# Seven block products instead of eight in the second feed-forward's up projection

## The chip, the cores and the metric

The kernel runs on one core of a Trainium2 chip. The time is the device time of one execution in microseconds; lower is better. TensorE (PE) multiplies matrices into PSUM, VectorE (DVE), ScalarE (ACT) and GpSimd (POOL) work on SBUF, the first two also on PSUM, and SyncE (SP) issues the loads.

## The reference

Two layers of a transformer over 512 latent tokens and 256 context tokens, model width 1024, float32. The first layer mixes by a state-space branch and attention, the second by latent attention (MLA); each ends with a gated feed-forward. What the change touches is the feed-forward of the second layer, which has only the 512 latent tokens:

```python
def swiglu(h, w_up, w_down):
    g, u = jnp.split(h @ w_up, 2, axis=-1)
    return (jax.nn.silu(g) * u) @ w_down
...
        x = x + mods[2] * o_lat
        h = modulate(rmsnorm(x, norm2_g[i]), mods[3], mods[4])
        x = x + mods[5] * swiglu(h, ffn_w_up[i], ffn_w_down[i])
...
    return rmsnorm(x, final_norm_g)
```

`w_up` is 1024 x 5632 (gate and up, 2816 hidden columns each), `w_down` is 2816 x 1024.

## The kernel before, in words

**Split products.** Every float32 matmul is made of three on TensorE: an operand is split into a high part (a copy rounded to the matmul's format, made by ScalarE) and a low part (the difference, made by VectorE or GpSimd), and high x high, high x low and low x high are added up in PSUM. For activations `Kern.split` does this (`L499`, `L500`; tiles `hh`, `hl`), for weights `WStream.split` (`L150` copies the loaded tile `wr` to `wh`, `L151` writes the difference `wl`; which engine does that alternates by the string `pat`).

**The weight stream.** `WStream` holds a plan of weight pieces in the order of their use. `dma` loads a piece of 128 x 1024 floats (512 KB), `split` makes its pair `wh`, `wl`. `lim(nraw, nhl)` says how many loaded pieces and how many pairs may be held; `free` gives a pair back and `pump` then loads and splits what comes next. All these tiles come from one pool of 14 buffers (`fp`).

**The second feed-forward** (`ffn` with `nt` = 4, called at the end of `phase_b`) goes through 11 blocks of 256 hidden columns, called pairs here (two tiles of 128 each), in four parts: (0, 1), (2, 3, 4), (5, 6, 7), (8, 9, 10). For each pair and each of its tiles `mm_w` fills two PSUM banks, one of gate and one of up, over eight contraction tiles, three matmuls each (`L662`, `L663`, `L665`), with the weight as stationary and all 512 tokens as moving operand. Pair 0 alone is done in two halves of 256 tokens, so that it can start when the first tokens are normalized. `act` then takes Silu of the gate (`L1248`), multiplies by up from PSUM (`L1249`) and splits the product into `hh` and `hl`. At the end of a part `out_gemm` multiplies these with the part's share of `w_down` (`gemm_t`, `L521` to `L523`) and adds the result, times a gate, to `x` (`L1188`, `L1189`); four matmul groups of the next part's first pair are started before it. After the last part, `final` normalizes and stores.

**Order.** The Python code names the instructions; a scheduler that simulates times puts them in order for each engine when the kernel is built, and on the chip every engine keeps this order. So an instruction that depends on nothing can be moved far ahead of its place in the code.

**Around it.** Before the feed-forward stands the attention output product, whose second half ends with `begin_norm` (normalize, transpose by `L248`, scale and shift by `L490`, split). The MLA stage earlier warms up the Exp table of ScalarE in `mla_in` (`L1325`), and its attention begins with `L1040`.

Of the kernel before, what the change touches and what calls it, by code (L numbers as in the profile page):

```python
# [18 lines left out]
P = 128  # L19
# [88 lines left out]
class WStream:  # L108
# [2 lines left out]

    def __init__(self, k, name):
        self.k, self.name = k, name
        self.plan = []
        self.raw, self.hl, self.rows = {}, {}, {}
        self.nd = self.ns = 0
        self.nraw, self.nhl = 2, 4
        self.live = 0
        self.pat = "P"
        self.stop = 1 << 30  # L120

    def add(self, srcs):
        i = len(self.plan)
        self.plan.extend(srcs)
        return list(range(i, len(self.plan)))

    def dma(self):
        src = self.plan[self.nd]
        t = self.k.f([P] + list(src.shape[1:]), F32, "wr")
        if isinstance(src, Halves):  # L130
            src.load(self.k.nc, t)
        else:
            self.k.nc.sync.dma_start(t, src)
        self.raw[self.nd] = t
        self.nd += 1

    def split(self):
        k, nc = self.k, self.k.nc
        i = self.ns
        if i >= self.nd:  # L140
# [12 lines left out]
        self.live += 1  # L153
        self.ns += 1
# [5 lines left out]
    def pump(self):  # L160
        while True:
            go = False
            while self.nd < min(len(self.plan), self.stop + self.nraw) and len(self.raw) < self.nraw:
                self.dma()
                go = True
            if self.ns < self.nd and self.live < self.nhl and self.ns < self.stop:
                self.split()
                go = True
            if not go:
# [14 lines left out]
class Kern:  # L184
# [393 lines left out]
    def plan_ffn(self, l):  # L578
        a, W, bp = self.a, self.W, self.block_pieces
        up, dn = a["ffn_w_up"][l], a["ffn_w_down"][l]  # L580
        pre = []
        for p, pairs in enumerate(FFN_PARTS):
            for j in pairs:
                gs = bp(up, 0, KD, 256 * j, 256, 4)
                self.i_up[l, j] = (pre + W.add(gs[len(pre):]), W.add(bp(up, 0, KD, HID + 256 * j, 256, 4)))
                pre = []
            if p + 1 < len(FFN_PARTS):

                pre = W.add(bp(up, 0, KD, 256 * FFN_PARTS[p + 1][0], 256, 4)[:1])
            self.i_dn[l, p] = [W.add(bp(dn, 2 * pairs[0], 2 * len(pairs), 512 * i, 512, 2)) for i in range(2)]  # L590

    def first_h(self):
# [708 lines left out]
            yield from self.out_gemm(hh, hl, 0, self.i_dn[l, p], range(nt), gate, after() if last else None)  # L1301


    def cq_at(self, s, i, t):
        return self.cqT[s][t // 2][:, i, (t % 2) * P:(t % 2 + 1) * P]

# [287 lines left out]
    def phase_b(self):  # L1594
# [51 lines left out]
        drive(self.out_gemm(self.oh, self.ol, 4, self.i_mo[1], range(NL), gate, self.begin_norm(1, 3)))  # L1646
        self.oh = self.ol = None
# [127 lines left out]
```

## Time and profile before

| | us |
|---|---|
| three timed runs | 2144.48, 2141.44, 2143.94 (median 2143.94) |
| the profiled execution's own time | 2144.06 |
| its span | 2142.1 |
| TensorE busy | 2053.3 (96%) |
| VectorE busy | 1217.9 (57%) |
| ScalarE busy | 842.9 (39%) |
| GpSimd busy | 798.9 (37%) |

Busy shares are averages over all stages. The second feed-forward runs from 1763 us to 2134 us of the span; what it waits for is read from that stretch alone. A matmul's row gives a start and a modelled duration that overlaps the next matmul; the distance of starts is what it costs in a stream.

### The profile page before, as it was taken

How to read it: one execution, taken by the hardware profiler on the slowest of the kernel's cores; microseconds unless marked ns; L12 is line 12 of the kernel's file. 1: busy time of each engine (PE TensorE's matmuls, PEld its weight loads, DVE VectorE, ACT ScalarE, POOL GpSimd, SP SyncE). 2: the span in 40 equal slices, each digit the busy share in tenths (PEclk: the TensorE clock that was granted, in tenths of full speed). 3: DMA queues.
4: the chain of work that ended last, by engine and by line, in shares of the span. 5: the costliest groups of instructions: out<-in, count | busy, mean ns of one | idle time of the engine just before them, and what ended most of it. 6: DMA issues, size and time to landing. Idle time of an engine off the chain costs nothing. (4 is left out here: it accounts for less than half of the span.)

```text
span 2142.1 us, 29547 instructions
## 1 busy us (share of the span) xinstructions
PE 2053.3 (96%) x11420; PEld 1689.4 (79%) x11420; DVE 1217.9 (57%) x2119; ACT 842.9 (39%) x1717; POOL 798.9 (37%) x701
## 2 busy tenths in 40 slices
PE   6999999999999899999999999999999999999998
PEld 3777777777777677888888878889888878888886
DVE  5699887867665697845345252175655663322223
ACT  4466554335665234312212212254555644222222
POOL 3456544575322355432232222254110154333333
PEclk9999999999999999999999999999999999999999
DMA  8211102410000641433335442112000033233232
GB/s 287 59 30 40 30 21 89 153 40 20 1 1 30 237 147 60 148 118 114 97 114 158 148 128 91 58 48 56 15 12 30 30 94 103 90 99 100 86 98 69
DMA packets 127574, 179.53 MB, mean 84 GB/s; under 512 B 16189, under 2 KB 77770, under 8 KB 127434
## 3 DMA queue, kind: packets, MB, share of 16 engines
q1 hardware_dynamic: 127434, 177.64, 26.3%
q8 instruction: 90, 1.47, 0.3%
q14 instruction: 50, 0.41, 0.1%
HBM read 172.35 MB, written 5.27 MB: 83 GB/s over the span
## 5 line engine op out<-in xcount | busy, mean ns | idle before, releaser
L151 POOL TENSOR_TENSOR wl<-wr,wh 128x1024 fp32r<-128x1024 f32 (+3 forms) x125 | 303.4, 2429 | 399.1 <-ACT wh L150 285.4
L150 ACT ACTIVATE wh<-wr 128x1024 fp32r<-128x1024 f32 (+3 forms) x211 | 218.5, 1037 | 517.4 <-DMA wr<-in_ffn_w_up_dram 126.2
L663 PE MATMUL gu<-hl,wh 128*128 128x512 f32 (+1 forms) x768 | 287.9, 375 | 1.5 <-POOL hl L500 1.5
L665 PE MATMUL gu<-hh,wl 128*128 128x512 f32 (+1 forms) x768 | 288.5, 376 | 0.4 <-DVE wl L151 0.4
L662 PE MATMUL gu<-hh,wh 128*128 128x512 f32 (+1 forms) x768 | 288.6, 377 | 0.0
L409 DVE SCALAR_TENSOR_TENSOR acc<-wa,sst,acc 128x512 f32<-128x512 f32 (+1 forms) x196 | 182.8, 975 | 88.1 <-DMA wa<-in_ada_w_dram 88.0
L151 DVE TENSOR_TENSOR wl<-wr,wh 128x1024 fp32r<-128x1024 f32 (+3 forms) x86 | 116.2, 1351 | 168.1 <-ACT wh L150 144.3
L521 PE MATMUL g<-wh,hh 128*128 128x512 f32 (+2 forms) x520 | 199.3, 384 | 0.5 <-DVE gt L1188 0.5
L522 PE MATMUL g<-wl,hh 128*128 128x512 f32 (+2 forms) x520 | 198.2, 381 | 0.0
L523 PE MATMUL g<-wh,hl 128*128 128x512 f32 (+2 forms) x520 | 197.2, 381 | 0.0
L1188 DVE TENSOR_TENSOR gt<-g,gate 128x512 f32<-128x512 f32 x132 | 90.3, 687 | 181.0 <-PE g L523 177.2
L662 PEld LDWEIGHTS gu<-hh,wh 128*128 128x128 f32 x768 | 144.4, 188 | 30.2 <-issue 2.8
L500 POOL TENSOR_TENSOR hl<-sg,hh 128x768 fp32r<-128x768 f32 (+1 forms) x44 | 71.8, 1631 | 249.3 <-ACT hh L499 249.1
L1038 DVE TENSOR_REDUCE nm<-S 128x1 f32<-128x768 f32 (+1 forms) x160 | 134.9, 848 | 45.5 <-PE S L1488 26.6
L663 PEld LDWEIGHTS gu<-hl,wh 128*128 128x128 f32 x768 | 144.8, 189 | 17.3 <-POOL hl L500 1.7
L665 PEld LDWEIGHTS gu<-hh,wl 128*128 128x128 f32 x768 | 144.9, 189 | 16.2 <-DVE wl L151 0.6
L1040 ACT ACTIVATE Pm<-S,nm 128x768 f32<-128x768 f32 (+1 forms) x160 | 130.2, 815 | 32.7 <-DVE nm L1038 32.0
L1189 POOL TENSOR_TENSOR x<-x,gt 128x512 f32<-128x512 f32 x66 | 90.6, 1378 | 132.1 <-DVE gt L1188 122.9
L248 PE MATMUL PTp<-ident,Pm 128*128 128x128 f32 x832 | 123.6, 276 | 6.1 <-ACT qT L1019 2.9
L248 PEld LDWEIGHTS PTp<-ident,Pm 128*128 128x128 f32 x832 | 96.1, 140 | 23.6 <-issue 10.4
L521 PEld LDWEIGHTS g<-wh,hh 128*128 128x128 f32 x520 | 97.6, 188 | 20.0 <-DVE gt L1188 1.0
L523 PEld LDWEIGHTS g<-wh,hl 128*128 128x128 f32 x520 | 97.7, 188 | 19.4
(308 smaller groups left out, 4657.9 us busy)
## 6 DMA issues: line engine op xcount, KB each, us to landing
wa<-in_ada_w_dram SPq DMA_DIRECT2D x96, 512.0 KB, 4.8
wr<-in_ffn_w_up_dram SPq DMA_DIRECT2D x88, 512.0 KB, 3.6
wr<-in_ffn_w_down_dram SPq DMA_DIRECT2D x44, 512.0 KB, 3.9
wr<-in_ab_w_in_dram SPq DMA_DIRECT2D x36, 512.0 KB, 3.7
wr<-in_ab_w_out_dram SPq DMA_DIRECT2D x16, 512.0 KB, 5.1
wr<-in_mla_w_o_dram SPq DMA_DIRECT2D x8, 512.0 KB, 3.7
yscr<-y SPq DMA_DIRECT2D x12, 256.0 KB, 2.6
yr<-yscr SPq DMA_DIRECT2D x6, 512.0 KB, 3.9
```

Source lines behind the costliest of these rows:

```text
L150: nc.scalar.activation(hi, raw, AF.Copy)
L151: eng.tensor_tensor(lo, raw, r32(hi), op=ALU.subtract)
L248: self.nc.tensor.transpose(out, in_, self.ident[:n, :n])
L409: nc.vector.scalar_tensor_tensor(acc[:, v], in0=raw[:, kk], scalar=c, in1=acc[:, v], op0=ALU.mult, op1=ALU.add)
L521: nc.tensor.matmul(ps, h, wh[:, kk, :], start=(n == 0), stop=False)
L522: nc.tensor.matmul(ps, h, wl[:, kk, :], start=False, stop=False)
L523: nc.tensor.matmul(ps, l, wh[:, kk, :], start=False, stop=(n == nk - 1))
L662: nc.tensor.matmul(o, a, hi[:, c0:c1], start=st, stop=False)
L663: nc.tensor.matmul(o, a, lo[:, c0:c1], start=False, stop=False)
L665: nc.tensor.matmul(o, b, hi[:, c0:c1], start=False, stop=sp)
L1038: nc.vector.tensor_reduce(nm, sp[:, 0:nb, 0:w], axis=AX.XY, op=ALU.max, negate=True)
L1040: nc.scalar.activation(p[:, 0:nkt * P].rearrange("p (a b) -> p a b", a=nb), sp[:, 0:nb, 0:w], AF.Exp, bias=nm, accum_out=u["sum"][:, ti, a ...
```

## The change

The up product of a pair is a product of two matrices that are each cut into 2 x 2 blocks: activations by tokens (256 + 256) and contraction (512 + 512), weights by contraction and by gate and up. Instead of eight block products the changed kernel makes seven, of sums and differences of blocks (Strassen's way, in the form with the fewest sums), and combines them. Pair 0 is computed as before; the ten others are changed.

- `begin_norm_q` takes the place of `begin_norm`: the normalized activations are kept whole (`hf`) and split by blocks ("11", "12", "21", "22": token half and contraction half). `sums_q` makes the four sums S1 to S4 in the course of pair 0, eight VectorE operations, and splits them.
- `WStream.seven` and `add_steps` plan seven steps for the four loaded pieces of a pair; `operand` makes the sum that a step needs on VectorE, in place, and `split` makes the pair from it. The low part of step n is written by the engine `PAT7[n]`: GpSimd for 0, 3, 5, VectorE for 1, 2, 4, 6.
- `up7` runs the seven products, 24 matmuls of 256 columns each (`mm_q`), and `ev` reads them out of PSUM: two copies on ScalarE, five additions on VectorE, the rest in SBUF.
- `ffn_q` takes the place of `ffn`. The stream may hold at most 14 buffers (`cap`), first 4 loaded pieces and 5 pairs, then 6 and 4 (before: 1 and 6). A Silu of one element is meant to load the table early.

```diff
+PAT7 = "PVVPVPV"
...
+    def operand(self, q, n):
+
+        a, b, d, c = (self.raw.get(i) for i in q["at"] + [None] * (4 - len(q["at"])))
+        V, G = self.k.nc.vector, self.k.nc.gpsimd
+        if n == 1:
+            V.tensor_tensor(b, d, b, op=ALU.subtract)
+        elif n == 2:
+            V.tensor_tensor(b, b, a, op=ALU.add)
+        elif n == 4:
+            V.tensor_tensor(a, d, b, op=ALU.subtract)
+        elif n == 5:
+            V.tensor_tensor(b, c, b, op=ALU.subtract)
+        for i in ((), (), (), (), (0,), (1, 3), (2,))[n]:
+            del self.raw[q["at"][i]]
+        return (a, b, b, c, a, b, d)[n]
...
-        raw = self.raw.pop(i)
+        raw = self.operand(q, n) if q else self.raw.pop(need)
         hi = k.f(list(raw.shape), F32R, "wh")
         lo = k.f(list(raw.shape), F32R, "wl")
-        eng = nc.gpsimd if self.pat[i % len(self.pat)] == "P" else nc.vector
+        pat = PAT7[n] if q else self.pat[i % len(self.pat)]
+        eng = nc.gpsimd if pat == "P" else nc.vector
...
+    def sums_q(self):
+
+        V, G = self.nc.vector, self.nc.gpsimd
+        self.quarters(("S1", "S2", "S3"))
+        for tt in range(2):
+            h1, h2 = self.hf[tt], self.hf[2 + tt]
+            a11, a12, a21, a22 = h1[:, 0:4], h1[:, 4:8], h2[:, 0:4], h2[:, 4:8]
+            V.tensor_tensor(a22, a21, a22, op=ALU.add)
+            V.tensor_tensor(a21, a11, a21, op=ALU.subtract)
+            self.split_q(a21, "S3", tt, G)
+            V.tensor_tensor(a11, a22, a11, op=ALU.subtract)
+            self.split_q(a11, "S2", tt, V)
+            self.split_q(a22, "S1", tt, G)
+            V.tensor_tensor(a12, a12, a11, op=ALU.subtract)
+            self.split_q(a12, "S4", tt, V)
+        self.hf = None
+
+    def mm_q(self, outs, i, name, start, stop):
+
+        nc = self.nc
+        wh, wl = self.W.get(i)
+        (h3, h1), (l3, l1) = self.q[name]
+        for o, m0 in outs:
+            for kk in range(4):
+                hi, lo = (h3[:, kk], l3[:, kk]) if kk < 3 else (h1, l1)
+                st, sp = start and kk == 0, stop and kk == 3
+                a, b = wh[:, kk, m0:m0 + P], wl[:, kk, m0:m0 + P]
+                nc.tensor.matmul(o, a, hi, start=st, stop=False)
+                nc.tensor.matmul(o, a, lo, start=False, stop=False)
+                nc.tensor.matmul(o, b, hi, start=False, stop=sp)
...
+    def up7(self, ids, hh, hl):
...
+        def ev(n, ps):
+            if n == 0:
+                t["p1"] = two(self.med(512, "hf"))
+                nc.scalar.activation(t["p1"], ps, AF.Copy)
+            elif n == 1:
+                t["w"] = self.e([P, 2, 2, 256], F32, "w7")
+                nc.scalar.activation(t["w"][:, 1], ps, AF.Copy)
+            elif n == 2:
+                t["u2"] = two(self.med(512, "hf"))
+                V.tensor_tensor(t["u2"], ps, t["p1"], op=ALU.add)
+            elif n == 3:
+                sg = t["sg"] = self.e([P, 2, 2, 256], F32, "sg7")
+                V.tensor_tensor(sg[:, :, 0], ps, t.pop("p1"), op=ALU.add)
+                nc.scalar.activation(sg[:, :, 0], sg[:, :, 0], AF.Silu)
+            elif n == 4:
+                w, u2 = t["w"], t["u2"]
+                V.tensor_tensor(w[:, 0], ps, u2, op=ALU.add)
+                G.tensor_tensor(u2, u2, w[:, 1], op=ALU.add)
+                G.tensor_tensor(w[:, 1], w[:, 1], w[:, 0], op=ALU.add)
+            elif n == 5:
+                sg = t["sg"]
+                V.tensor_tensor(sg[:, :, 1], ps, t.pop("u2"), op=ALU.add)
+                nc.scalar.activation(sg[:, :, 1], sg[:, :, 1], AF.Silu)
+                G.tensor_tensor(sg[:, :, 1], sg[:, :, 1], t["w"][:, 1], op=ALU.mult)
+            else:
+                sg, w = t.pop("sg"), t.pop("w")
+                V.tensor_tensor(w[:, 0], ps, w[:, 0], op=ALU.add)
+                V.tensor_tensor(sg[:, :, 0], sg[:, :, 0], w[:, 0], op=ALU.mult)
+                for m in range(2):
...
+        for n, name in enumerate(("11", "S3", "S2", "12", "S1", "22", "S4")):
...
+    def ffn_q(self, l, gate, after):
+        nc = self.nc
+        nc.scalar.activation(self.small(1, "ex"), self.one[:, 2:3], AF.Silu)
...
+                    self.W.lim(6, 4)
+                else:
+                    yield from ahead or self.up7(ids, hh, hl)
...
-        W.lim(1, 6)
+        W.cap = 14
+        W.lim(4, 5)
         gate = [self.gate(1, 5, 0)]
-        drive(self.ffn(1, NL, gate, self.final))
+        drive(self.ffn_q(1, gate, self.final))
```

The built order shows where the work now stands. Line numbers of the changed kernel are its own: there `L152` to `L158` are the sums of `operand`, `L188` and `L189` the copy and the difference of a weight (before `L150`, `L151`), `L1452` to `L1470` lines of `ev`, `L540` the low part of an activation (before `L500`).

VectorE, pair 3, which stands in the middle of part 2. Before, between the gate products of two of its tiles:

```order
L1249 TENSOR_TENSOR sg_17302<-sg_17302,gu_17253 128x512
L151 TENSOR_TENSOR wl_17335<-wr_17244,wh_17334 128x1024
L151 TENSOR_TENSOR wl_17371<-wr_17344,wh_17370 128x1024
L1249 TENSOR_TENSOR sg_17382<-sg_17382,gu_17309 128x512
L1249 TENSOR_TENSOR sg_17438<-sg_17438,gu_17389 128x512
```

And of the change, from the eviction of its product 2 to that of its product 6 (`hf_17562` is the sum after product 2, `w_17529` and `sg_17592` hold up and gate):

```order
L152 TENSOR_TENSOR wr_17322<-wr_17491,wr_17322 128x1024
L1452 TENSOR_TENSOR hf_17562<-gu_17531,hf_17493 128x512
L189 TENSOR_TENSOR wl_17557<-wr_17252,wh_17556 128x1024
L1459 TENSOR_TENSOR w_17529<-gu_17595,hf_17562 128x512
L1455 TENSOR_TENSOR sg_17592<-gu_17531,hf_17493 128x2x256
L189 TENSOR_TENSOR wl_17622<-wr_17322,wh_17621 128x1024
L154 TENSOR_TENSOR wr_17322<-wr_17322,wr_17289 128x1024
L1464 TENSOR_TENSOR sg_17592<-gu_17595,hf_17562 128x2x256
L156 TENSOR_TENSOR wr_17289<-wr_17491,wr_17322 128x1024
L189 TENSOR_TENSOR wl_17654<-wr_17322,wh_17653 128x1024
L1469 TENSOR_TENSOR w_17529<-gc_17660,w_17529 128x512
```

The sums and differences of the next pair's weights now stand between the evictions of this pair's products.

GpSimd, the same pair. Before:

```order
L151 TENSOR_TENSOR wl_17341<-wr_17338,wh_17340 128x1024
L500 TENSOR_TENSOR hl_17386<-sg_17382,hh_17385 128x512
L151 TENSOR_TENSOR wl_17377<-wr_17374,wh_17376 128x1024
L500 TENSOR_TENSOR hl_17442<-sg_17438,hh_17441 128x512
L151 TENSOR_TENSOR wl_17477<-wr_17474,wh_17476 128x1024
```

And of the change, one pair's turn:

```order
L189 TENSOR_TENSOR wl_17522<-wr_17104,wh_17521 128x1024
L1460 TENSOR_TENSOR hf_17562<-hf_17562,w_17529 128x512
L189 TENSOR_TENSOR wl_17589<-wr_17289,wh_17588 128x1024
L1461 TENSOR_TENSOR w_17529<-w_17529 128x512
L1466 TENSOR_TENSOR sg_17592<-sg_17592,w_17529 128x2x256
L189 TENSOR_TENSOR wl_17686<-wr_17525,wh_17685 128x1024
L540 TENSOR_TENSOR hl_17692<-sg_17592,hh_17691 128x512
```

Three differences of weights and four operations of 512 columns make up its turn, instead of two and two.

ScalarE, in the MLA input stage after the first feed-forward, where `L1325` before and `L1553` of the change load the Exp table. One piece of the difference there would repeat the rows around it, so the rows of the change alone:

```order
L1553 ACT_TABLE_LOAD
L1553 ACTIVATE ex_12999<-ss_12993 128x1
L1491 ACT_TABLE_LOAD
L1491 ACTIVATE ex_16557<-one_78 128x1
L1572 ACTIVATE shared_12965<-g_13002 128x32
L1550 ACTIVATE mc_13038,ss_13039<-g_13002 128x256
```

The Silu warm-up `L1491` of `ffn_q` has come here from the second feed-forward; before, `L1344` (now `L1572`) followed the Exp warm-up at once. A further table load stands before attention's first exponential.

## Rows read from the trace of the kernel before

**Rows 1.** The page: engines' busy time, then the span in 40 slices.

```profile
span 2142.1 us, 29547 instructions
PE 2053.3 (96%) x11420; PEld 1689.4 (79%) x11420; DVE 1217.9 (57%) x2119; ACT 842.9 (39%) x1717; POOL 798.9 (37%) x701
...
PE   6999999999999899999999999999999999999998
...
PEclk9999999999999999999999999999999999999999
```

**Rows 2.** TensorE's waits, 1763 to 2134 us: waiter, releaser, total, times, longest.

```profile
PE gu L663 <- POOL hl L500: 1.5, 1, 1.5
```

**Rows 3.** TensorE's timeline in two streams: start, duration, engine, line, operation.

```profile
1776.00 0.28 PE L665 MATMUL gu<-hh,wl 128*128 128x256 f32 x1
...
1788.18 0.28 PE L662 MATMUL gu<-hh,wh 128*128 128x256 f32 x1
...
1942.23 0.39 PE L663 MATMUL gu<-hl,wh 128*128 128x512 f32 x1
...
2003.22 0.39 PE L665 MATMUL gu<-hh,wl 128*128 128x512 f32 x1
```

**Rows 4.** Busy time by stretch: part 3's up products, then its down products.

```profile
core 0: us, PE busy (x) PEld busy (x) DVE busy (x) ACT busy (x) POOL busy (x), PEclk, DMA share, GB/s
...
1942.00:2003.00 61.00, 61.00 (x265) 49.41 (x264) 14.09 (x14) 19.89 (x24) 20.90 (x12) 1.00 0.33 104
2003.00:2042.00 39.00, 39.00 (x170) 31.58 (x169) 11.58 (x13) 6.36 (x6) 13.58 (x8) 1.00 0.26 79
```

**Rows 5.** Groups by line and shape, 1789 to 2134 us: total, mean ns; idle before.

```profile
L151 POOL TENSOR_TENSOR wl<-wr,wh 128x1024 fp32r<-128x1024 f32 x30 | 72.1, 2403 | 97.7 <-ACT wh L150 83.9 <-PE g L523 9.1 <-PE gu L663 4.8
...
L150 ACT ACTIVATE wh<-wr 128x1024 fp32r<-128x1024 f32 x59 | 62.6, 1060 | 177.0 <-DMA wr<-in_ffn_w_up_dram 113.6 <-DMA wr<-in_ffn_w_down_dram 36.2 <-POOL wl L151 27.1
...
L151 DVE TENSOR_TENSOR wl<-wr,wh 128x1024 fp32r<-128x1024 f32 x29 | 41.7, 1438 | 77.9 <-ACT wh L150 64.9 <-PE gu L663 12.5 <-PE g L522 0.5
...
L1189 POOL TENSOR_TENSOR x<-x,gt 128x512 f32<-128x512 f32 x16 | 20.7, 1294 | 37.4 <-DVE gt L1188 37.4
L1249 DVE TENSOR_TENSOR sg<-sg,gu 128x512 f32<-128x512 f32 x21 | 14.5, 688 | 80.3 <-ACT sg L1248 79.8
L499 ACT ACTIVATE hh<-sg 128x512 fp32r<-128x512 f32 x21 | 13.2, 628 | 12.7 <-DVE sg L1249 12.7
L1248 ACT ACTIVATE sg<-gu 128x512 f32<-128x512 f32 x21 | 12.5, 597 | 40.6 <-PE gu L665 40.6
...
L1668 DVE TENSOR_TENSOR xn<-x,fg 128x512 f32<-128x512 f32 x7 | 4.8, 688 | 6.7 <-ACT xn L466 6.7
```

**Rows 6.** VectorE's timeline, 1847 to 1871 us.

```profile
1847.42 0.69 DVE L1188 TENSOR_TENSOR gt<-g,gate 128x512 f32<-128x512 f32 x1 [1.36 <-PE g L523]
...
1857.83 1.23 DVE L151 TENSOR_TENSOR wl<-wr,wh 128x1024 fp32r<-128x1024 f32 x1 [0.26 <-ACT wh L150]
...
1869.93 1.89 DVE L151 TENSOR_TENSOR wl<-wr,wh 128x1024 fp32r<-128x1024 f32 x1 [1.23 <-PE gu L663]
```

**Rows 7.** GpSimd's timeline, 1845 to 1871 us.

```profile
1846.00 2.41 POOL L151 TENSOR_TENSOR wl<-wr,wh 128x1024 fp32r<-128x1024 f32 x1 [9.11 <-PE g L523]
...
1858.39 1.82 POOL L500 TENSOR_TENSOR hl<-sg,hh 128x512 fp32r<-128x512 f32 x1 [1.46 <-ACT hh L499]
...
1869.44 1.30 POOL L500 TENSOR_TENSOR hl<-sg,hh 128x512 fp32r<-128x512 f32 x1 [6.12 <-ACT hh L499]
```

**Rows 8.** The page's DMA issues: target, source, queue, count, KB each, us to landing.

```profile
wr<-in_ffn_w_up_dram SPq DMA_DIRECT2D x88, 512.0 KB, 3.6
```

**Rows 9.** ScalarE's timeline in the MLA stage: the Exp table load, the first exponential.

```profile
1439.83 1.28 ACT L1325 ACT_TABLE_LOAD   x1
...
1497.06 0.90 ACT L1040 ACTIVATE Pm<-S,nm 128x768 f32<-128x768 f32 x1 [0.32 <-DVE nm L1038]
```

**Rows 10.** TensorE's timeline in the MLA input stage, around the Exp table load.

```profile
1441.38 0.44 PE L248 MATMUL mT<-ident,mc 128*128 128x128 f32 x2 [2.13 <-DVE mc L1326]
```

More of the change, by code (lines that the diff above doesn't have):

```diff
@@ L162, in pump @@
             go = False
-            while self.nd < min(len(self.plan), self.stop + self.nraw) and len(self.raw) < self.nraw:
+            last = self.src[self.stop][0] + self.nraw if self.stop < len(self.src) else len(self.loads)
+            while self.nd < min(len(self.loads), last) and len(self.raw) < self.nraw and 2 * self.live + len(self.raw) < self.cap:
                 self.dma()
                 go = True
-            if self.ns < self.nd and self.live < self.nhl and self.ns < self.stop:
+            if self.ns < min(len(self.plan), self.stop) and self.src[self.ns][0] < self.nd and self.live < self.nhl \
+                    and 2 * self.live + 2 + len(self.raw) <= self.cap:
                 self.split()
@@ L580, in plan_ffn @@
         up, dn = a["ffn_w_up"][l], a["ffn_w_down"][l]
-        pre = []
+        pre, q = [], None
         for p, pairs in enumerate(FFN_PARTS):
@@ new lines, in begin_norm_q, with norm, after @@
+    def begin_norm_q(self, l, ch):
+        nc = self.nc
+        self.q, self.hf = {}, [None] * NL
+        self.quarters(("11", "12", "22"))
+        self.quarters(("21", "S4"))
+        A, B = self.mod[l][:, ch + 1, 0, :], self.mod[l][:, ch, 0, :]
+        live = {}
+        def norm(xn, t):
+            hf = self.hf[t] = self.e([P, KD, P], F32, "hfT")
+            for h in range(2):
+                ps = self.ps("nT", [P, 4, P])
+                for i in range(4):
+                    kt = 4 * h + i
+                    self.tr(ps[:, i, :], xn[:, kt * P:(kt + 1) * P])
+                for i in range(4):
+                    kt = 4 * h + i
+                    nc.vector.tensor_scalar(hf[:, kt, :], ps[:, i, :], A[:, kt:kt + 1], B[:, kt:kt + 1], op0=ALU.mult, op1=ALU.add)
+                self.split_q(hf[:, 4 * h:4 * h + 4], f"{t // 2 + 1}{h + 1}", t % 2, nc.gpsimd if h else nc.vector)
+        def after(t, nb):
+            if nb == 0:
+                live[t] = self.f([P, D], F32, "xn"), self.small(2, "s2")
+            xn, s2 = live[t]
+            self.norm_half(self.x[t], xn, s2, nb)
+            if nb == 0:
+                return None
+            del live[t]
+            nc.scalar.activation(xn, self.x[t], AF.Copy, scale=self.rstd2(s2))
+            return lambda: norm(xn, t)
+        return after
@@ new lines, in ffn_q @@
+    def ffn_q(self, l, gate, after):
+        nc = self.nc
+        nc.scalar.activation(self.small(1, "ex"), self.one[:, 2:3], AF.Silu)
+        ahead = None
+        hh, hl = [], []
+        for p, pairs in enumerate(FFN_PARTS):
+            for j in pairs:
+                ids = self.i_up[l, j]
+                if j == 0:
+                    gu = [self.ps("gu", [P, 2, 512]) for _ in range(2)]
+                    for s in range(2):
+                        if s:
+                            self.sums_q()
+                        for x in range(2):
+                            for k in range(2):
+                                yield from self.mm_q([(gu[m][:, x, 256 * s:256 * s + 256], m * P) for m in range(2)],
+                                                     ids[x][k], f"{s + 1}{k + 1}", k == 0, k == 1)
+                                if s:
+                                    self.W.free(ids[x][k])
+                    del self.q["21"]
+                    for m in range(2):
+                        sg = self.s([P, TA], F32, "sg")
+                        nc.scalar.activation(sg[:, 0:TL], gu[m][:, 0, :], AF.Silu)
+                        nc.vector.tensor_tensor(sg[:, 0:TL], sg[:, 0:TL], gu[m][:, 1, :], op=ALU.mult)
+                        h, lo = self.s([P, TA], F32R, "hh"), self.s([P, TA], F32R, "hl")
+                        self.split(sg[:, 0:TL], h[:, 0:TL], lo[:, 0:TL])
+                        hh.append(h)
+                        hl.append(lo)
+                    self.W.lim(6, 4)
+                else:
+                    yield from ahead or self.up7(ids, hh, hl)
+                    ahead = None
+            last = p == len(FFN_PARTS) - 1
+            nxt = [], []
+            if last:
+                self.q = None
+            else:
+                ahead = self.up7(self.i_up[l, FFN_PARTS[p + 1][0]], *nxt)
+                yield from islice(ahead, 5)
+            yield from self.out_gemm(hh, hl, 0, self.i_dn[l, p], range(NL), gate, after() if last else None)
+            hh, hl = nxt
```

75 lines of the change are left out of this document (66 added, 9 removed).

## The prediction

> **What bounds the kernel now.** I read the page first: TensorE is busy for 96% of the span at the full granted clock, and in the slices of the second feed-forward (from 1763 us, the last seven) it shows 9 in all but the very last, which holds the tail [rows 1]. So I asked TensorE's waits for this stretch: one wait of 1.5 us at its very start and nothing else up to 2134 us [rows 2]. The stretch is a pure stream of matmuls. Its price is the distance between two starts, not the "busy" of one, which overlaps its neighbours: 264 matmuls of 512 columns from 1942.23 to 2003.22 are 60.99/263 = 0.232 us apart, and 104 of 256 columns from 1776.00 to 1788.18 are 12.18/103 = 0.1183 us apart [rows 3]. Two narrow ones cost 0.2366, hardly more than a wide one. VectorE, ScalarE and GpSimd have air: in the 61 us of the up stretch of part 3 they work 14.1, 19.9 and 20.9 us [rows 4]. Whatever takes matmuls out of this stream shortens the kernel, as long as nobody becomes late in handing TensorE its operands. That second half is the whole question.
>
> **TensorE's saving.** A pair of hidden tiles (one j) takes 8 contraction tiles x 3 matmuls (high x high, high x low, low x high) x 2 tiles x 2 (gate, up) = 96 matmuls of 512 columns, 22.27 us. Seven products of 2 x 4 x 3 = 24 matmuls of 256 columns are 168, 19.87 us. Saved: 2.40 us a pair. Pair 0 stays classical, ten pairs change: **-24.0 us**. The down products and the tail behind the last matmul are the same instructions.
>
> **What a pair asks of the other engines instead.** Durations are in [rows 5].
> - Weights: seven splits instead of four, so seven ScalarE copies of 1.06 us, four differences on VectorE and three on GpSimd (the pattern of the diff), and four sums on VectorE that are 128x1024 from two SBUF operands, like the difference; unblocked that takes 1.23 us there and 2.40 on GpSimd [rows 6, 7].
> - Results: five VectorE additions from PSUM at 0.69, a product and a split of 512 columns in SBUF at 0.69 each (as the product in SBUF at `L1668` does); on GpSimd two additions, a product and a split at 1.29.
> VectorE: 8 x 1.23 + 7 x 0.69 = 14.7 us. GpSimd: 3 x 2.40 + 4 x 1.29 = 12.4. ScalarE: 7 x 1.06 + 6 x 0.62 = 11.1. Each fits into 19.87.
>
> **But two of them share something.** At 1869.93 a VectorE difference took 1.89 instead of 1.23 us, because a GpSimd subtraction had begun at 1869.44 and ended at 1870.74: an overlap of 0.81 cost 0.66. At 1857.83 VectorE came first and kept its 1.23; GpSimd's 1.29 became 1.82 [rows 6, 7]. So the later one stands still, except for some 0.15 us at its beginning. An eviction whose one operand is PSUM isn't touched: at 1847.42 it took 0.69 wholly inside a GpSimd split [rows 6, 7]. Hence I count the time on this common path as the duration less 0.15: 1.08 and 0.54 for VectorE's wide and narrow operations with two SBUF operands, 2.25 and 1.14 for GpSimd's. A pair asks for 8 x 1.08 + 2 x 0.54 + 3 x 2.25 + 4 x 1.14 = **21.0 us**, more than TensorE's 19.87. (Before: two splits each side and two small ones, 9 us of 22.27.)
> The Trainium skill ("SBUF — State Buffer", Who interferes with whom) says that a VectorE operation with two SBUF inputs and a GpSimd operation take a shared port pair for the whole instruction, the second fully blocked. By "whole instruction" a pair would ask for 23.6 us, by the rows for 21.0: the trace agrees on the blocking, not on the whole.
>
> Nor is the path always in use. Twice a pair GpSimd's next job in order waits for a VectorE eviction from PSUM (`L1460` for `L1452`, `L1466` for `L1464`), and meanwhile neither uses it: 2 x 0.69 = 1.4. So a long row of pairs would run at some 22.4 us each, which is no gain at all over 22.27.
>
> **Why there is still a gain.** The pairs come in parts of 1 (after pair 0), 3, 3 and 3, and between parts lie down products: in 39 us there the two engines work 11.6 and 13.6 us [rows 4], so the queues start each part on time. Four weight pairs are held, so three products (3 x 24 x 0.1183 = 8.5 us) lie between a free buffer and its next use; the chain of a step is sum 1.23, copy 1.06, difference 1.23, some 0.3 between engines = 3.8. Slack 4.7. In three pairs the path falls behind by 3 x (22.4 - 19.87) = 7.6, so TensorE waits 7.6 - 4.7 = **2.9 us a part**, 8.7 in three parts. Bounds: with 21.0 a pair the lag is 3.4 and nothing waits (0); with a GpSimd difference in the chain that is blocked once (1.23 + 1.06 + 2.40 + 0.3 + 2.25 = 7.2) the slack is 1.3 and a part waits 6.3 (18.9). The value is nearest to the unblocked row, which most of the 29 VectorE splits show (their mean is 1.44 against 1.23 [rows 5]).
> Loads are as many as before and land in 3.6 us [rows 8]. The sum `L152` needs a load whose buffer the step before has just left, and eviction `L1452` stands behind it in VectorE's order; it comes 8.5 us after the last product's eviction, so this is covered as long as VectorE isn't late, and is in the bounds above.
>
> **Smaller terms.** (a) Pair 0 also hides the sums of the activations: eight VectorE operations of 512 columns and four splits on either engine, 12 x 0.54 + 4 x 1.14 = 11 us of the path beside the weights of pair 1, under 192 x 0.1183 = 22.7 us of matmuls. I take **+1** (0 to 4). The 1.5 us wait at the start may go or stay; it is left as it is (-1.5 to 0). (b) At the end of a part the last product's chain (two 0.69, copy 0.63, split 1.29, plus VectorE's lag of up to 4.7) is covered by the next part's first product, 2.84 us, and the first two down tiles on finished tiles, 24 x 0.232 = 5.6; half a microsecond at each of four ends, **+2** (0 to 7). Holding four instead of six weights in the down products is in it. (c) The added Silu warm-up depends on nothing, and the order puts it into the MLA input stage, right behind the Exp warm-up: one table load more there, and one more before attention's first exponential. A load takes 1.28 us [rows 9]. TensorE had just waited 2.1 us in the first place [rows 10], and before the first exponential ScalarE was idle for 0.32 us only [rows 9]. One of the two counts: **+1.3** (0 to 2.6).
>
> **Sum** against the profiled execution's own 2144.06 us (2142.1 of span and 2.0 around it; the median of the three timed runs is 2143.94, 0.1 less): -24.0 + 8.7 + 1 + 2 + 1.3 = -11.0, **2133 us**. Its own range is 2124 to 2143.
>
> **Rivals.**
> 1. *The operands are always in time.* The path is shared more cleverly than I think and the slack takes the rest. Speaks for it: 21.0 against 19.87 makes only 3.4 us of lag a part. Against: VectorE's queue is fixed and a wait for PSUM holds up the next weight. -24.0 + about 0: 2120 us.
> 2. *The slack is nearly gone from the start.* If the differences of a chain are usually blocked (the bound of 1.3 us above), a part waits 6.3 us, and -24.0 + 18.9 + 4.3 is next to nothing: 2143 us. For it: before the change a VectorE difference is already blocked often enough to bring its mean to 1.44 [rows 5], with half the traffic. Against: between parts the queues start afresh.
> 3. *The other side: whole durations exclude each other.* Then a pair takes 11.2 + 12.4 = 23.6 us, and ten pairs add 13.3, with the small terms (b) and (c) 2144.06 + 13.3 + 3.3 = 2161 us. (This is what the reading of the Trainium skill's page named above would come to.) It decides as soon as the two engines together need over 22.27 us a pair. For it: blocked pieces pass their delay to a fixed order in both queues. Against: the rows show 0.15 us of each blocked operation running free, and evictions from PSUM unhindered.
> That the change doesn't do what it says isn't among them: the order shows 168 matmuls a pair.
>
> **Chances.** My case 0.45, rival 1 0.17, rival 2 0.20, rival 3 (with milder forms from 2149 up) 0.18. The range from 2119 to 2151 us holds my case, rival 1 but for 0.02, rival 2 and the mild end of rival 3: 0.8. About 0.2% (4.3 us) is what a measurement of this kernel can tell from no change. Faster than 2139.7: 0.43 + 0.17 + 0.02 = 0.62. Within: 0.02 + 0.15 + 0.03 = 0.20. Slower than 2148.2: 0.03 + 0.15 = 0.18.
>
> **What would show it.** In the changed profile, 256-column up matmuls 0.118 us apart without idle time inside a product (else the saving is mis-sized). TensorE's waits, none before, should be some 3 us a part, on weight differences of VectorE or GpSimd, and fall into the second and third pair of a part, hardly into the first. VectorE's differences and sums should have means clearly above 1.23, GpSimd's above 2.40; if they stay at these, rival 1. If the first pairs of parts already last over 22 us, rival 2 or 3. The prediction is wrong if the waits stand at another place: at the ends of parts, at the change from pair 0 to pair 1, or before `L248` in the MLA stage behind the table loads.

## The result and the profile after

The changed kernel takes 2160.23 us (median of four runs, 2159.62 to 2162.02), the kernel before 2142.69 in the same session (2139.62 to 2144.48): a ratio of 1.0085, interval [1.0067, 1.0102]. It is slower by 17.5 us, where 11 us less was forecast.

The page of the changed kernel answers to [rows 1]. TensorE's busy time fell by only 4.6 us, the span grew by 18.1, and the line of slices has an 8, seventh from its end, where it had a 9:

```profile
span 2160.2 us, 31324 instructions
...
PE 2048.7 (95%) x12140; PEld 1720.5 (80%) x12140; DVE 1379.3 (64%) x2237; ACT 885.3 (41%) x1770; POOL 885.3 (41%) x731
...
PE   6999999999999899999999999999999998999998
```

TensorE's waits in the second feed-forward answer to [rows 2], where one wait of 1.5 us stood (waiter, releaser, total, times, longest):

```profile
PE gu L1430 <- DVE hf L1452: 9.6, 5, 2.8
PE gu L1430 <- DVE sg L1512: 5.3, 1, 5.3
PE gu L1432 <- DVE wl L189: 4.3, 4, 1.5
PE g L563 <- POOL hl L540: 3.0, 2, 1.9
PE g L561 <- DVE gt L1239: 1.1, 2, 0.6
PE gu L1430 <- ACT q L1367: 1.0, 1, 1.0
PE g L562 <- POOL wl L189: 0.8, 2, 0.5
```

With three smaller ones it is 26.3 us. The largest item isn't a weight but an eviction, `L1452`: the first matmul of product 3 (`gu<-q`, the quarter 12) waits until product 2 has been read out of PSUM. Both are halves of one two-bank tile, and the wait is for the tile: with a tile of its own for product 3 (a run below) 3.4 of the 9.6 us are left. Why the eviction is late is seen in VectorE's timeline (start, duration, idle before) and, in the second fence, GpSimd's:

```profile
1875.09 1.21 DVE L189 TENSOR_TENSOR wl<-wr,wh 128x1024 fp32r<-128x1024 f32 x1
1876.49 1.50 DVE L540 TENSOR_TENSOR hl<-sg,hh 128x512 fp32r<-128x512 f32 x1 [0.20 <-ACT hh L539]
1878.60 2.73 DVE L152 TENSOR_TENSOR wr<-wr,wr 128x1024 f32<-128x1024 f32 x1 [0.60 <-DMA wr<-in_ffn_w_up_dram]
1881.25 0.68 DVE L1452 TENSOR_TENSOR hf<-gu,hf 128x512 f32<-128x512 f32 x1
```

```profile
1875.96 1.48 POOL L540 TENSOR_TENSOR hl<-sg,hh 128x512 fp32r<-128x512 f32 x1 [1.35 <-ACT hh L539]
1877.47 2.77 POOL L189 TENSOR_TENSOR wl<-wr,wh 128x1024 fp32r<-128x1024 f32 x1
```

The sum `L152` waits 0.60 for its load, then takes 2.73 instead of 1.23 us, because GpSimd's difference runs until 1880.24. The eviction behind it runs at its 0.68. TensorE, out of work since 1879, starts at 1881.98, and then something that the prediction doesn't have. TensorE's timeline:

```profile
1878.82 0.29 PE L1431 MATMUL gu<-qc,wh 128*128 128x256 f32 x1
1878.95 0.28 PE L1432 MATMUL gu<-qc,wl 128*128 128x256 f32 x1
1881.98 0.58 PE L1430 MATMUL gu<-q,wh 128*128 128x256 f32 x1 [2.76 <-DVE hf L1452]
...
1882.58 0.41 PE L1432 MATMUL gu<-q,wl 128*128 128x256 f32 x1
...
1887.70 0.41 PE L1432 MATMUL gc<-qS,wl 128*128 128x256 f32 x1
...
1888.25 0.28 PE L1432 MATMUL gu<-q,wl 128*128 128x256 f32 x1
1888.36 0.28 PE L1430 MATMUL gu<-q,wh 128*128 128x256 f32 x1
```

From 1882.58 to 1887.70 the 25 matmuls are 0.213 us apart instead of 0.118. The windows (last three columns: granted clock, DMA share, GB/s) say why: the lower of the two levels, 1.2 GHz, is granted for most of it. (The Trainium skill, "TensorE: Matmul & The Clock Gate", What's actually happening, calls the throttled clock the default, which activity releases; the rows agree as to the two levels.) Before the change the whole stretch from 1763 to 2134 us was granted 1.00 (first row; the others are of the changed kernel).

```profile
1763.00:2134.00 371.00, 369.51 (x1697) 303.90 (x1695) 112.69 (x145) 109.40 (x151) 137.49 (x87) 1.00 0.30 95
...
1804.00:1810.00 6.00, 5.37 (x26) 5.37 (x27) 1.27 (x3) 3.30 (x6) 4.80 (x3) 0.53 0.66 237
1880.00:1888.00 8.00, 6.02 (x28) 6.02 (x29) 4.15 (x5) 0.86 (x2) 4.44 (x4) 0.58 0.31 96
1983.00:1988.00 5.00, 4.75 (x27) 4.75 (x28) 2.02 (x4) 0.16 (x1) 2.93 (x2) 0.66 0.36 108
2086.00:2090.00 4.00, 4.00 (x23) 4.00 (x23) 1.02 (x3) 0.30 (x1) 3.05 (x2) 0.57 0.40 134
```

Each of the four stands right behind a wait of 5.3 or 2.8 us. Length times the missing share of the clock: 6 x 0.47 + 8 x 0.42 + 5 x 0.34 + 4 x 0.43 = 9.6 us (10.2 if the whole stretch is summed in windows of 8 us).

So the feed-forward, first up matmul to last down matmul: 371.3 before, less its wait of 1.5, less 24.0, plus 26.3 of waits, plus 9.6 of clock = 381.7; measured are 385.5 (1766.94 to 2152.41). The distances of starts close this gap. In the four stretches the matmuls lie 2.3, 2.8, 1.6 and 1.6 us further apart in sum than at 0.118, which is 8.4 and not 9.6, as the windows also cover idle time before the restart. And each of the 20 waits costs some 0.24 us beyond its listed length, 4.8 in all: the list counts from the modelled end of the matmul before, 0.28 us behind its start (from 1878.95 to 1881.98 it is 3.03 us, not 2.76 + 0.12), and the first matmul behind a wait takes about 0.1 more. So 345.8 + 26.3 + 8.4 + 4.8 = 385.3. Ahead of the feed-forward the changed kernel is 3.9 us later (1766.94 against 1763.04), and the tail is the same: 14.2 + 3.9 = 18.1. In the traces of the runs below, with the warm-up and without, this start lies between 1760 and 1766, so the 3.9 hold for these two executions alone.

The groups by line and shape, 1767 to 2152 us, answer to [rows 5] (total, mean ns, idle before); VectorE's first, then GpSimd's:

```profile
L189 DVE TENSOR_TENSOR wl<-wr,wh 128x1024 fp32r<-128x1024 f32 x52 | 88.1, 1693 | 25.7 <-ACT wh L188 12.0 <-POOL wl L189 8.8 <-PE g L562 3.2
...
L1470 DVE TENSOR_TENSOR sg<-sg,w 128x512 f32<-128x512 f32 x10 | 20.5, 2048 | 0.1
...
L1452 DVE TENSOR_TENSOR hf<-gu,hf 128x512 f32<-128x512 f32 x10 | 6.8, 681 | 2.7 <-PE gu L1432 2.7
```

```profile
L189 POOL TENSOR_TENSOR wl<-wr,wh 128x1024 fp32r<-128x1024 f32 x42 | 114.0, 2715 | 51.1 <-ACT wh L188 46.5 <-issue 1.5 <-ACT hf L1446 1.2
```

Two SBUF operands: a product of 512 columns takes 2.05 us on average, three times its 0.69. One PSUM operand, same shape: 0.68, as ever. So the shared path is real and works as described; what it costs TensorE was mis-sized.

### The profile page after: what moved, and what is told of

Read it like the earlier page. It is cut to its first block, busy times and chain, and to the rows that moved or that the text cites. A ratio compares the mean times of both kernels' runs of the same rounds, so it can differ in the third digit from the quotient of the medians.

```text
span 2160.2 us, 31324 instructions
## 1 busy us (share of the span) xinstructions
PE 2048.7 (95%) x12140; PEld 1720.5 (80%) x12140; DVE 1379.3 (64%) x2237; ACT 885.3 (41%) x1770; POOL 885.3 (41%) x731
## 5 line engine op out<-in xcount | busy, mean ns | idle before, releaser
L189 POOL TENSOR_TENSOR wl<-wr,wh 128x1024 fp32r<-128x1024 f32 (+3 forms) x135 | 339.9, 2519 | 349.8 <-ACT wh L188 246.4
L188 ACT ACTIVATE wh<-wr 128x1024 fp32r<-128x1024 f32 (+3 forms) x241 | 249.8, 1039 | 513.5 <-PE g L562 185.0
L189 DVE TENSOR_TENSOR wl<-wr,wh 128x1024 fp32r<-128x1024 f32 (+3 forms) x106 | 160.7, 1516 | 109.1 <-ACT wh L188 91.7
L713 PE MATMUL gu<-hh,wh 128*128 128x512 f32 (+1 forms) x384 | 144.5, 377 | 0.0
L716 PE MATMUL gu<-hh,wl 128*128 128x512 f32 (+1 forms) x384 | 144.3, 376 | 0.0
L714 PE MATMUL gu<-hl,wh 128*128 128x512 f32 (+1 forms) x384 | 144.1, 376 | 0.0
L540 POOL TENSOR_TENSOR hl<-sg,hh 128x768 fp32r<-128x768 f32 (+1 forms) x34 | 60.4, 1778 | 175.3 <-ACT hh L539 175.3
L288 PEld LDWEIGHTS PTp<-ident,Pm 128*128 128x128 f32 x832 | 96.2, 141 | 23.6 <-issue 10.4
L562 PEld LDWEIGHTS g<-wl,hh 128*128 128x128 f32 x520 | 98.5, 189 | 19.3 <-POOL wl L189 1.7
L561 PE MATMUL g<-wh,h1h 128*128 128x512 f32 x240 | 98.7, 412 | 4.3 <-DVE zt L964 4.3
L1103 POOL COPY rb<-rc 128x256 f32<-128x256 f32 x40 | 15.9, 398 | 211.7 <-DVE rc L1101 211.7
```

The source lines that it names most:

```text
L288: self.nc.tensor.transpose(out, in_, self.ident[:n, :n])
L561: nc.tensor.matmul(ps, h, wh[:, kk, :], start=(n == 0), stop=False)
L562: nc.tensor.matmul(ps, h, wl[:, kk, :], start=False, stop=False)
L713: nc.tensor.matmul(o, a, hi[:, c0:c1], start=st, stop=False)
L714: nc.tensor.matmul(o, a, lo[:, c0:c1], start=False, stop=False)
L716: nc.tensor.matmul(o, b, hi[:, c0:c1], start=False, stop=sp)
```

## The experiments

In five sessions, each beside the kernel before. Line numbers are each run's own. "The feed-forward" is first up to last down matmul of the profiled execution; "clock" is the sum, over windows of 8 us, of length times missing clock. Two theories went in. A: the waits come from shared PSUM tiles, so the tiles are the fault. B: VectorE and GpSimd don't keep up on their shared path, and the tile is only where it shows.

**No warm-up.** `ffn_q` without its first line.

```
-        nc.scalar.activation(self.small(1, "ex"), self.one[:, 2:3], AF.Silu)
```

> Leaves out the Silu warm-up of `ffn_q` (L1491), nothing else. Read from the changed trace: the two table loads that it causes (1440.34, and 1498.48 before attention's first exponential) shift everything behind them from -0.99 to +3.92 us against before, because TensorE waits and its next matmuls are granted half the clock. If that is so: 2160.2 - 4.9 = 2155.3, with the whole gain ahead of the feed-forward. By the prediction's own term (c): -1.3, 2158.9. If the loads were hidden: 2160.

Measured 2157.85 us, 1.0065 [1.0047, 1.0082]: 2.4 less, between the first two figures, with overlapping intervals. ScalarE's timelines show it, the changed kernel first:

```profile
1438.83 1.28 ACT L1553 ACT_TABLE_LOAD   x1
1440.34 1.28 ACT L1491 ACT_TABLE_LOAD   x1
...
1498.48 1.28 ACT L1091 ACT_TABLE_LOAD   x1
1499.78 0.90 ACT L1091 ACTIVATE Pm<-S,nm 128x768 f32<-128x768 f32 x1
```

```profile
1436.09 1.28 ACT L1552 ACT_TABLE_LOAD   x1
...
1494.12 0.90 ACT L1091 ACTIVATE Pm<-S,nm 128x768 f32<-128x768 f32 x1 [0.32 <-DVE nm L1089]
```

From the Exp load to the first exponential it is 60.95 us with the warm-up, 58.03 without, 57.23 before [rows 9]. In all five traces with the warm-up it is 60.0 to 61.5 us, in the thirteen of the change without it 58.0 to 58.4. So the two loads cost 2.9 us, not 4.9. The rest of the delay fits the clock there (0.66 from 1440 to 1445), but no run shows it by itself. TensorE's wait of 2.1 us in the MLA input stage [rows 10] is in both kernels; in the profiled execution of before full clock followed it, in that of the changed kernel the lower level.

**Product 3 in a tile of its own**, and the same with product 2 moved as well. Of the change's tiles remains one line:

```
-            if n in (0, 1, 6):
-                ps = two(self.ps("gc" if n else "g", [P, 512]))
...
+            ps = two(self.ps("g gc gu gc gu gu g".split()[n], [P, 512]))
```

> Only the PSUM tiles change: products 2 and 3 (and 4 and 5) no longer share one two-bank tile, product 3 goes to `gc`, product 6 to `g`, 2, 4 and 5 each take a `gu` tile. Theory A (product 3 waits for the eviction L1452 of product 2 only because both lie in one tile, and L1452 stands late in VectorE's queue): the 9.6 us of waits on L1452 go, and so does the half clock behind them (2.8 + 1.6 + 1.4 us); some comes back as waits on weights; 2146 to 2152. Theory B (the prediction's: VectorE and GpSimd fall behind on their shared path, the wait only shows at this place): the same microseconds turn up as waits on weight differences, 2156 to 2161.

> As the run with its own tile for product 3, and product 2 goes to `g` as well, so that pair 1 needs the tiles of pair 0 two products (5.7 us) later. Theory A: besides the waits on L1452, the 5.3 us wait on pair 0's product L1512 goes, and the 2.2 us of half clock behind it: 2139 to 2146. Theory B: waits on weight differences take their place, 2152 to 2160.

Measured 2152.64 (1.0043 [1.0027, 1.0059]) and 2150.35 (1.0039 [1.0021, 1.0057]). Waits of the first:

```profile
PE g L561 <- DVE w L1469: 6.2, 3, 2.6
PE gu L1430 <- DVE sg L1507: 3.6, 1, 3.6
PE gu L1430 <- DVE hf L1452: 3.4, 3, 2.2
```

The waits on `L1452` fall from 9.6 to 3.4, and 6.2 turn up at the eviction of product 6, which a down product now waits for: product 6 lies in `g` here, a tile of the down products, so this cost is the edit's own. In all 22.4 us instead of 26.3, and 5.1 of clock instead of 10.2 by this count. The time lies between the two ranges, 0.6 us above A's: the shared tile cost something, but far from all. The second run missed both ranges too. Its profiled execution, at 2157.13 the slowest of five, has 21.2 us of waits, 9.1 of them on product 6.

**The first sum without its load.**

```
-            V.tensor_tensor(b, d, b, op=ALU.subtract)
+            V.tensor_tensor(b, a, b, op=ALU.subtract)
```

> The first weight sum of a pair (L152) takes the first piece instead of the third, so that it no longer waits for the load that comes last; the same number, size and engine of operations (what is computed differs in this sum). Theory A with the load as the reason why L1452 is late (VectorE stands 0.6 us for the load at 1878.0 and then collides with GpSimd's difference until 1881.3): waits on L1452 shrink from 9.6 us to under 3, 2148 to 2153. Theory B, or VectorE late for other reasons: 2157 to 2161.

Measured 2160.1 (1.0077 [1.006, 1.0095]): no gain. The waits on `L1452` fall to 0.8 and move, whole, to weights:

```profile
PE gu L1432 <- DVE wl L189: 9.3, 5, 3.0
PE gu L1430 <- DVE sg L1512: 5.3, 1, 5.3
```

So the load made `L1452` late, but it isn't the root. In this run, beside GpSimd's operations, `L1470` takes 2.89 us at 1870.73 and the difference of a weight 2.29 at 1874.68, and TensorE waits 2.9 us for that difference.

**All products in tiles of their own, no warm-up** (`g gc gc g gu gu gc`), and a version with product 2 in `gu`:

> Without the Silu warm-up, and each product in a PSUM tile of its own: products 0 and 3 in `g`, 1, 2 and 6 in `gc`, 4 and 5 in `gu`, so that no product waits for the eviction of the one before, pair 1 leaves pair 0's tiles alone for three products, and the down products don't wait for the eviction of product 6 (6.2 us with three waits where product 6 lay in `g`). Theory A (PSUM tiles): TensorE's waits on evictions go, the feed-forward takes some 365 to 372 us (385.5 in the changed kernel), 2136 to 2143. Theory B (the shared path of VectorE and GpSimd): what goes there comes back as waits on weight differences, 374 to 380 us, 2145 to 2152.

> As the other, but product 2 lies in `gu`: pair 1 meets pair 0's tiles after two products again. Against the other it tells what that one place is worth. Theory A: 3.6 us of wait and some half clock, 3 to 6 us more than the other. Theory B: the same time as the other, within 2 us.

Measured 2153.13 (1.0044 [1.0029, 1.0059]) and 2155.36 (1.0053 [1.0037, 1.007]). No wait on another product's tile is left in the first but one of 0.5 us; its feed-forward still takes 381.7 us, with 23.3 of waits:

```profile
PE g L561 <- ACT hh L539: 5.3, 3, 3.4
PE g L562 <- POOL wl L189: 5.1, 2, 4.1
PE g L563 <- POOL hl L540: 3.0, 3, 2.0
```

13.4 us of these stand at the ends of parts, on the last pair's splits and on down weights that queue behind them. That is B in kind, 1.1 us above its range and at another place again. The second version, 2.2 us longer, can't be told apart from the first. The first kernel is the base of what follows.

**Less work on the path, from either side.** GpSimd's additions and product on one column, or three of VectorE's sums on one column, in this manner:

```
-                G.tensor_tensor(u2, u2, w[:, 1], op=ALU.add)
+                G.tensor_tensor(u2[:, :, 0:1], u2[:, :, 0:1], w[:, 1, :, 0:1], op=ALU.add)
```

```
-            V.tensor_tensor(b, b, a, op=ALU.add)
+            V.tensor_tensor(b[:, :, 0:1], b[:, :, 0:1], a[:, :, 0:1], op=ALU.add)
```

> The kernel with the tiles `g gc gc g gu gu gc` and no warm-up, but GpSimd's two additions and one product of a pair (L1460, L1461, L1466) are done on one column of each half only: same order, same waits between engines, a pair asks 3 x 1.14 = 3.4 us less of the path that VectorE and GpSimd share (17.6 instead of 21.0, under TensorE's 19.87); VectorE has exactly the same instructions. What is computed is not the reference's. Theory B (shared path): VectorE's means fall (differences from some 1.7 towards 1.4) and the waits on weights go, 8 to 15 us faster than the kernel that does the whole additions. If VectorE's own 14.7 us, the order of its queue or the latency of a chain are the limit: within 3 us of it.

> As the same kernel, but three of VectorE's four weight sums of a pair (L154, L156, L158) are done on one column of each piece: 3 x 1.08 = 3.2 us less of the shared path (17.8), and VectorE's own time falls from 14.7 to about 11.4. What is computed is not the reference's. Theory B: nearly the same gain as with GpSimd's short additions, 8 to 15 us. If VectorE's own time or order is the limit: a gain here and none there. If neither helps: the waits have another cause (loads, the chain from split to matmul).

Measured 2132.54 (0.9938 [0.9922, 0.9954]) and 2142.42 (0.9992 [0.9982, 1.0001]): 20.6 and 10.7 us less than the base. With GpSimd's operations short, VectorE, whose instructions are untouched, speeds up (base, then this run; its `L189` from 1798 to 1500 too, while `L158`, now beside GpSimd's difference, goes from 1844 to 2286):

```profile
L1470 DVE TENSOR_TENSOR sg<-sg,w 128x512 f32<-128x512 f32 x10 | 16.7, 1666 | 0.1
```

```profile
L1470 DVE TENSOR_TENSOR sg<-sg,w 128x512 f32<-128x512 f32 x10 | 8.4, 844 | 0.1
```

In both runs the waits inside the last three parts are gone. Left are ends of parts; with VectorE's sums short these are still 11 us, on GpSimd's work for the most part:

```profile
PE g L562 <- POOL wl L189: 4.9, 2, 3.9
PE g L561 <- ACT hh L539: 3.2, 2, 2.2
PE g L563 <- POOL hl L540: 2.6, 3, 1.6
```

So the gains aren't equal, as B had it (the first is above its 8 to 15), and the ends of parts depend on GpSimd's queue besides.

**Both at once**, which prices TensorE's saving:

> The kernel with its own PSUM tiles and without the warm-up, and both cuts at once: GpSimd's two additions and one product and three of VectorE's weight sums of a pair on one column each. A pair then asks some 14.4 us of the shared path against TensorE's 19.87. What is computed is not the reference's. It prices TensorE's saving by itself: if the step of 24.0 us is right, the feed-forward takes 371.3 - 24.0 - 1.5 = 345.8 us and what is left of waits at the ends of parts (3 to 6 us): 349 to 352, 2120 to 2125. If narrow matmuls cost more than 0.118 us in this place, or the waits are not the path's: over 356 us, 2130.

Measured 2127.64 (0.9921 [0.9904, 0.9938]), feed-forward 355.8. Its waits are 5.7, its clock costs 3.4 (granted 0.57 from 1821 to 1829): 371.3 - 1.5 - 24.0 + 5.7 + 3.4 = 354.9. The 24.0 hold within 1 us; the time of 2120 to 2125 was missed by 2.6, which the clock accounts for.

**More cover at the ends of parts, and smaller parts.** `add_steps(q, (0, 1))` and `islice(ahead, 10)` put two products ahead; the other runs cut the parts to (0,1), (2,3), (4,5), (6,7), (8,9,10), or do both.

> The kernel with its own PSUM tiles and without the warm-up, and two products of the next part (instead of one) ahead of the down products of a part. It gives the last product of a part 2.84 us more cover. In that kernel TensorE still waits 13 us at the ends of parts (3.4 + 2.0, 1.0 + 1.0, 0.9 + 0.6, 4.1 + 0.4), on splits of the hidden tiles and of down weights. Theory B with the ends as the place where a part's lag is paid: 6 to 9 us of these go, and some half clock: 2143 to 2148. If the lag is only carried on into the next part: 2150 to 2154.

> The kernel with its own PSUM tiles and without the warm-up, with parts (0,1), (2,3), (4,5), (6,7), (8,9,10) instead of (0,1) and three times three: the same products and down matmuls, eight more evictions and additions into x. Theory B (VectorE falls behind pair by pair and catches up in the down products): a part of two pairs ends before the lag is up, waits inside parts go (4 us), but there is one more end of a part at 1.5 to 4.5 us: 2150 to 2155. If the ends are dear because of the third pair's lag, they become cheap too: 2143 to 2148.

> Both: smaller parts and two products ahead. Theory B: the sum of both effects, 2140 to 2146, at best level with the kernel before; the shared path (21.0 us a pair against 19.87) leaves no more.

Measured 2153.91 (1.0046 [1.0031, 1.0061]), 2163.86 (1.0097 [1.0082, 1.0112]) and 2158.48 (1.0065 [1.005, 1.008]). The first lies in the range of its second case, the two others missed. Two ahead moves the waits from the splits to weights that now come late. With smaller parts each of the five ends costs 4.1 to 5.2 us of wait, where the base has 5.7, 2.0, 1.8 and 4.5 at its four, and the clock comes on top: 18.8 us. The two cheap ends of the base stand behind a third pair; those of this run, but for the last, stand behind a second one.

**All differences on VectorE.**

```
-PAT7 = "PVVPVPV"
+PAT7 = "VVVVVVV"
```

> The kernel with its own PSUM tiles and without the warm-up, and all seven weight differences of a pair on VectorE (none on GpSimd). GpSimd's work falls from 12.4 to 5.2 us a pair unblocked, VectorE's rises from 14.7 to 18.4; the shared path asks 21.0 - 3 x (2.25 - 1.08) = 17.5 us. If GpSimd's own queue is what fails to keep up: 10 us or more faster than 2153, 2140. If VectorE with the time that GpSimd holds it up is the limit: in the run with short GpSimd operations and in the one without, VectorE was held up by some 0.46 us for each microsecond of GpSimd's work on the path, so 18.4 + 0.46 x 4.6 = 20.5 us a pair against 19.95 now and TensorE's 19.87: as slow or slower, 2153 to 2160.

Measured 2132.49, 0.9941 [0.9923, 0.9959]: 20.6 less than its base, faster than before the change. The waits are 8.3 us, 2.7 of them in pair 0 and the rest at ends of parts:

```profile
PE g L563 <- POOL hl L540: 2.4, 2, 2.0
PE g L562 <- POOL wl L189: 2.3, 1, 2.3
PE g L1432 <- DVE wl L189: 1.7, 1, 1.7
```

VectorE, with the most work of all runs, isn't the limit; the estimate of 20.5 us for it was no good guide. GpSimd's queue alone isn't either: the short sums took the waits inside parts away and left its instructions as they were. What all three edits lower is the demand on the path: from 21.0 us a pair to 17.8 (short sums), 17.6 (short GpSimd operations) and 17.5 (this run), each below TensorE's 19.87.

**Every other pair in eight products**, with smaller parts and two ahead:

> Smaller parts, two products ahead, own PSUM tiles, no warm-up, and only pairs 2, 4, 6, 8 and 10 in seven products; 0, 1, 3, 5, 7 and 9 in eight (256-column matmuls like pair 0). TensorE saves 5 x 2.4 - 5 x 0.44 = 9.8 us against before. Theory B: VectorE has 22.7 us for about 8 us of work in every other pair, nothing falls behind, few waits and little half clock: 2133 to 2138. If ends of parts cost 2 to 3 us each whatever VectorE does: 2143 to 2148.

> The same with pair 1 in seven products too (0, 3, 5, 7, 9 in eight): 2.4 + 0.44 us less of matmuls, but pair 1 stands behind the sums of the activations and at the end of part 0, where the changed kernel waited 5.3 us and the one with its own tiles 1.5 + 5.3. Theory B: 2 to 6 us slower than the other; without such a wait 2.8 us faster.

Measured 2154.88 (1.0043 [1.0027, 1.0059]) and 2146.28 (1.0009 [1.0, 1.0018]). The first missed: pair 1 in eight products takes both `gu` tiles of pair 0 at once and waits 5.6 us for its product. The second is level with before: it gives up four of the ten pairs and still waits 11.2 us, half of it at the ends of its five parts. It missed as well: 8.6 us faster than the first, which has that one wait.

**The one line alone on the changed kernel**, and the best version with two products ahead:

> The changed kernel with one line edited: all seven weight differences of a pair on VectorE. Products 2 and 3 still share a PSUM tile, the warm-up is in. If the shared path was the root and the shared tile only the place where it showed: nearly the whole gain, 2132.5 + 2.5 to 5 (warm-up) + 3 to 5 (pair 0's product before pair 1): 2137 to 2143. If the shared tile costs by itself: above 2146.

> All differences on VectorE, own PSUM tiles, no warm-up, and two products ahead at the ends of parts. There TensorE still waited 2.0 + 0.4 and 2.3 + 0.4 us, with some 3 us of half clock behind. If cover is what is missing: 2126 to 2130. With PVVPVPV one product more ahead gave nothing (2153.9 against 2153.1), since the next part's weights were late instead; if that holds here too: 2131 to 2136.

Measured 2137.17 (0.9964 [0.9952, 0.9976]) and 2134.15 (0.9951 [0.9936, 0.9966]). With warm-up and shared tiles left in, the one line gives 23 us (26 by the ratios, as the kernel before took 3 us longer beside this run). The waits on `L1452` are nearly gone, though the tile is still shared, and the time lies at the edge of the range for the shared path:

```profile
PE g L563 <- POOL hl L540: 3.1, 2, 1.9
PE gu L1430 <- DVE sg L1512: 3.1, 1, 3.1
...
PE gu L1430 <- DVE hf L1452: 0.6, 2, 0.4
```

One product more ahead gives nothing, as the second case had it.

## Why the prediction was wrong

- **TensorE's saving, -24.0: right**, by the run with both cuts. In the changed kernel the third pairs of parts take 19.84 and 19.80 us from product 0 to the next product 0 (1893.32 to 1913.16, 1993.39 to 2013.19).
- **Two engines on one path: right in kind.** Differences on VectorE mean 1.69, on GpSimd 2.72, evictions 0.68, as the last part asked. The 0.15 us hold too: at 1872.28 a product `L1470` took 2.88, and GpSimd's difference overlapped it by 2.33: 2.88 - 2.33 - 0.69 leaves -0.14.
- **The waits of 2.9 us a part: the step that failed first**, in size and place, though its own bounds (0 to 18.9 in all) held the sum. It spread a pair's work evenly over three pairs. But the sums of a pair are made while TensorE is at the pair before: beside the second pair of part 2 VectorE was busy 22.3 of 27.3 us, beside the third, with down weights next, 12.4 of 19.9. So the second pair is overloaded and the third runs free. And the slack was counted on weights alone (three products), while evictions stand in the same queue with a slack of one product. TensorE goes from product 2 to 4 and then to 3, which needs `L1452`; product 4 alone lies between, 2.84 us. The text saw `L1452` behind `L152`, and called it covered "as long as VectorE isn't late". Inside parts this came to 14.1 us (9.6 + 4.3 + 0.2) instead of 8.7.
- **Each wait priced at its own length: the step that failed by most.** The prediction had no term for what follows a wait. Measured are 8.4 us of matmuls at the lower clock (9.6 by the windows) and 4.8 us at the 20 restarts, 13.2 in all.
- **The small terms.** (a) pair 0 to pair 1: 5.3 us instead of +1, outside its 0 to 4, on pair 0's product in VectorE's queue, and 2.3 of slow matmuls behind. (b) ends of parts: about 6 us instead of +2, within 0 to 7. (c) the warm-up: 2.9 instead of 1.3, just outside its bounds, both loads counting.
- **The balance.** The span grew by 18.1 us where -11.0 was forecast. Of the 29.1 between, the waits inside parts make 5.4, pair 0 to pair 1 4.3, the ends of parts 3.9, what follows the waits 13.2, and the stretch ahead of the feed-forward 2.6 (3.9 in these two executions instead of 1.3); the wait at the start gives 0.5 back.
- **Rival 3 gave 2161, close to the result, by another mechanism.** Not every pair took 23.6 us; third pairs ran at 19.8, and with the same pattern but own tiles and no warm-up the time was 2153. That its number is near is luck. Its ground, too much on the shared path, is what the runs confirm. The Trainium skill's "whole instruction" ("SBUF — State Buffer", Who interferes with whom) stays 0.14 us off the row above.
- **What stays open:** how the 10 us between the run with short sums and the one with short GpSimd operations divide between GpSimd's queue and the clock (6.9 us in one, 1.7 in the other).

## What to carry to other kernels

When two engines share a path, price an operation by what it holds of that path: by the prediction's estimate from rows a difference on GpSimd held it 2.25 us, the same on VectorE 1.08. So giving the idler engine work made both late, and moving three differences to the engine with more work gained 23 us. Find each queue's tightest customer, an eviction rather than a weight here, and take the peak of a period, not its mean. When a stream of matmuls that had no waits gets them, price the long ones at more than their length: here waits of 2.8 us brought 1.6 to 2.8 us of slow matmuls each, one of 5.3 us 2.3.

## What the runs showed of the hardware

- After a wait of 2.8 us TensorE's matmuls were 0.213 us apart for 5.1 us, at a granted clock of 0.58 from 1880 to 1888, then 0.118 again; after one of 5.3 us the window of 6 us had 0.53. In the run with smaller parts the missing clock sums to 18.8 us in windows of 8 us, beside 26.8 of waits.
- It doesn't follow each wait. The one of 1.9 us at 1830.23 was followed by full clock up to 1836. The one of 2.1 us in the MLA input stage was followed by full clock in the profiled execution of before, and by 0.66 over 5 us (1440 to 1445) in that of the changed kernel. Up to there the two run the same matmuls.
- Even a tiny operation waits for the path. In the run with short GpSimd operations a product of 128x2 at 1860.63 took 1.09 us beside a VectorE difference that ran from 1860.45 to 1861.67; an addition of the same size just ahead of one, at 1875.92, took 0.19.
